# Six extra short TensorE passes, in two groups, in the last third of a two-layer streaming encoder

## The chip, the cores and the metric

The kernel runs on one core of a Trainium2 chip. The metric is the device time of one execution in microseconds (us). The input arrays are laid out on the host beforehand and are no part of the time.

## The reference, cut to what matters

272 tokens (16 learned ones and 256 of the input) of width 2048 pass two layers. Layer 0 is a Mamba-2 mixer and a SwiGLU feed-forward. Then one shared K/V is projected, and layer 1 is a stick-breaking attention and a second SwiGLU feed-forward. The part around the change is this:

```python
def stick_breaking_attention(u, w_q, k, v, w_o):
    ...
    return o @ w_o

def swiglu(u, w_gate_up, w_down):
    gu = u @ w_gate_up
    return (jax.nn.silu(gu[..., :FFN_HIDDEN]) * gu[..., FFN_HIDDEN:]) @ w_down

# layer 1
h = h + stick_breaking_attention(u, sb_w_q[j], k_shared, v_shared, sb_w_o[j])
h = h + swiglu(rmsnorm(h, norm_ffn[layer]), ffn_gate_up[layer], ffn_down[layer])
return rmsnorm(h, final_norm)[:, N_META:]
```

All of it is float32; D_MODEL is 2048 (16 blocks of 128), FFN_HIDDEN is 5632 (44 blocks of 128).

## The kernel before, in words

Activations lie transposed: 128 features on the partitions, tokens along the free dimension (272 of them in layer 0 and in K/V, 256 from the query projection on). Every weight matrix is streamed once from HBM in chunks of 128 x 1024 (`load`, tile `raw`, 5 buffers, on SyncE's queue).

To keep float32 accuracy at the speed of the fp32r type, each weight chunk is split by `halves` into a rounded part `hi` (ScalarE, L105, 5 buffers) and a remainder `lo` (VectorE, L107, 4 buffers), and the activations are kept as two such parts as well (`pair`, `split_scaled`). One 128 x 128 block of a product is then three matmul passes in PSUM (`mac`): hi by the low part of x (L120), hi by its high part (L121), lo by its high part (L122). Each pass has its own weight load (LDWEIGHTS), also of 128 x 128.

`project` makes one output tile: 16 blocks (44 in the down projection) by three passes, all into one PSUM tile of the pool `pp` (tag "pp", 4 buffers). `project_block` makes several output tiles at once, one chunk of eight blocks of each in turn, and calls `pump()` after each chunk; `pump` advances the generators in `side`, which hold the small work of the last attention heads (`attend`: transposes L551 to L553 and L576 to L580, scores L560 and L561, the product with V L586 to L588). `rstd` makes a row norm with plain float32 matmuls (L180) in a PSUM tile of the pool `pr` (one buffer).

The end of the kernel, which the change touches, is in this order: for each of 16 heads the K, V and query tiles with `attend` woven in (the query tile reads `uq`, 256 columns); then the attention's output projection `w_o` on `ob` (256 columns), whose first `FILLERS` = 4 tiles go through `project_block` and the other 12 through `project`, one by one; then `ffn(1, ...)` on `u` (256 columns), whose first four tiles (gate 0, up 0, gate 1, up 1) go through `project_block` with `rstd` after the first half, then gate and up of m = 2 to 43 through `project`, then the down projection on `hid`; then a short tail with the final norm.

TensorE takes its passes in program order. Nothing else orders the work around the change than the program order and the waits on the buffers named above. The ten passes at L202 at the very start of the kernel write a `pr` tile (`wake`) that nobody reads either.

Of the kernel before, what the change touches and what calls it, by code (L numbers as in the profile page):

```python
# [6 lines left out]
F32 = mybir.dt.float32  # L7
# [6 lines left out]
P = 128  # L14
# [22 lines left out]
FILLERS = 4  # L37
# [8 lines left out]
def trunk(tc, a, out):  # L46
    nc = tc.nc
    V, S, PE = nc.vector, nc.scalar, nc.tensor

    with tc.tile_pool(name="const", bufs=1) as cp, \  # L50
# [38 lines left out]
        def nm(s):  # L89
            uid[0] += 1  # L90
            return f"{s}_{uid[0]}"


        def load(src, k0, n, m=P):
            raw = wp.tile([P, LC, P], F32, tag="raw", name=nm("raw"), bufs=RAW)
            b0 = k0 // LC * LC
            b1 = min(b0 + LC, src.shape[0] // (P * m))
            piece = src[b0 * P * m:b1 * P * m].rearrange("(p k c) -> p k c", p=P, c=m)
            nc.sync.dma_start(raw[:, :n, :m], piece[:, k0 - b0:k0 - b0 + n, :])
            return raw  # L100


        def halves(raw, n, m=P):
            hi = wp.tile([P, WC, P], F32R, tag="hi", name=nm("hi"), bufs=5)
            S.copy(hi[:, :n, :m], raw[:, :n, :m])  # L105
            lo = wp.tile([P, WC, P], F32R, tag="lo", name=nm("lo"), bufs=4)
            V.tensor_tensor(out=lo[:, :n, :m], in0=raw[:, :n, :m],  # L107
                            in1=hi[:, :n, :m].bitcast(F32), op=ALU.subtract)
            return hi, lo


        def pair(pool, K, n, pad, step, tail=0, **kw):
            t = pool.tile([P, pad + 2 * K * step + tail], F32R, **kw)
            t = t[:, pad:pad + 2 * K * step].rearrange("p (s k t) -> p s k t", s=2, t=step)
            return [t[:, i, :, :n] for i in range(2)]

        def mac(ps, hi, lo, j, x, k, first, last, m=P):
            n = x[0].shape[-1]
            wh, wl, xh, xl = hi[:, j, :m], lo[:, j, :m], x[0][:, k, :], x[1][:, k, :]
            PE.matmul(ps[:, :n], wh, xl, start=first, stop=False)  # L120
            PE.matmul(ps[:, :n], wh, xh, start=False, stop=False)  # L121
            PE.matmul(ps[:, :n], wl, xh, start=False, stop=last)  # L122

        def project(src, x, m=P, o=None, then=None):
            K = x[0].shape[1]
            if o is None:
                o = pp.tile([P, 512], F32, tag="pp", name=nm("pp"))
            o = o[:m]
            for k0 in range(0, K, WC):
                c = min(WC, K - k0)  # L130
                if k0 % LC == 0:
                    raw = load(src, k0, min(LC, K - k0), m)
                hi, lo = halves(raw[:, k0 % LC:], c, m)
                for j in range(c):
                    mac(o, hi, lo, j, x, k0 + j, k0 + j == 0, k0 + j == K - 1, m)
                if k0 == 0 and then:
                    then()
            return o

        def project_block(srcs, x, then=None):  # L140
            K = x[0].shape[1]
            pss = [pp.tile([P, 512], F32, tag="pp", name=nm("pp")) for _ in srcs]
            for k0 in range(0, K, WC):
                c = min(WC, K - k0)
                for ps, src in zip(pss, srcs):
                    hi, lo = halves(load(src, k0, c), c)
                    for j in range(c):
                        mac(ps, hi, lo, j, x, k0 + j, k0 + j == 0, k0 + j == K - 1)
                    pump()
                if k0 == 0 and then:  # L150
                    then()
            return pss

        def times(dst, ps, r):
            V.tensor_tensor(out=dst, in0=ps[:, :r.shape[-1]], in1=r, op=ALU.mult)  # L155

        def residual(hm, ps):
            V.tensor_tensor(out=hm, in0=ps[:, :hm.shape[-1]], in1=hm, op=ALU.add)  # L158

        def split_scaled(dst, k, src, gcol):  # L160
            S.activation(dst[0][:, k, :], src, AF.Identity, scale=gcol)
            V.scalar_tensor_tensor(out=dst[1][:, k, :], in0=src, scalar=gcol,
                                   in1=dst[0][:, k, :].bitcast(F32),
                                   op0=ALU.mult, op1=ALU.subtract)
# [10 lines left out]
        def rstd(dst, acc, width, more=()):  # L175
            n = acc.shape[-1]
            ps = prp.tile([P, 512], F32, tag="pr", name=nm("pr"))
            parts = [acc, *more]
            for i, part in enumerate(parts):
                PE.matmul(ps[:, :n], ones, part, start=i == 0, stop=i == len(parts) - 1)  # L180
            sd = sp.tile([P, T], F32, tag="ms", name=nm("sd"), bufs=1)[:, :n]
            S.activation(sd, ps[:, :n], AF.Sqrt, bias=epst, scale=1.0 / width)
            V.reciprocal(dst, sd)
# [14 lines left out]
        u = pair(upool, KD, T, PAD["u"], TP, 16, tag="u", name="u0")  # L198
# [4 lines left out]
        for k, c in PIECES:  # L203
# [11 lines left out]
            hi, lo = halves(raw, GT * c)  # L215
# [6 lines left out]
        with tc.tile_pool(name="ssd0", bufs=1) as q0, \  # L222
# [13 lines left out]

            with tc.tile_pool(name="dtp", bufs=1) as dq:
                psd = project(a["w_dt"], u, m=NH, o=ptp.tile([P, 512], F32, tag="pt", name=nm("pt")),
                              then=lambda: rstd(rB, acc, D))[:, :T]
                for j in range(GT):  # L240
# [237 lines left out]
            u = pair(upool, KD, T, PAD["u"], TP, 16, tag="u", name="u1")  # L478
# [4 lines left out]
        def ffn(layer, u, t0, finish):  # L483
            n = T - t0
            with tc.tile_pool(name=f"ffn{layer}", bufs=1) as fp, \
                    tc.tile_pool(name=f"fft{layer}", bufs=2) as ft:
                gu, dn = a["w_gu"][layer], a["w_down"][layer]
                r = rB[:, t0:]
                pre = project_block([gu[0], gu[KF], gu[1], gu[KF + 1]], u,
                                    lambda: rstd(r, acc[:, t0:], D))  # L490
                for f0, f1 in PARTS[layer]:
                    hid = pair(fp, PARTS[layer][0][1], n, PAD["hid"][layer], TP if layer == 0 else SEQ,
                               tag="hid", name=nm(f"hid{layer}"))
                    hid = [v[:, :f1 - f0] for v in hid]
                    for m in range(f0, f1):
                        gt = ft.tile([P, n], F32, tag="gt", name=nm("gt"))
                        times(gt, pre.pop(0) if pre else project(gu[m], u), r)
                        S.activation(gt, gt, AF.Silu)
                        ut = ft.tile([P, n], F32, tag="ut", name=nm("ut"))
                        times(ut, pre.pop(0) if pre else project(gu[KF + m], u), r)  # L500
                        V.tensor_tensor(out=ut, in0=ut, in1=gt, op=ALU.mult)
                        S.copy(hid[0][:, m - f0, :], ut)
                        V.tensor_tensor(out=hid[1][:, m - f0, :], in0=ut, in1=hid[0][:, m - f0, :].bitcast(F32),
                                        op=ALU.subtract)
                    done = finish if f1 == KF else lambda m, ps: residual(h[:, m, t0:], ps)
                    srcs = [dn[m][f0 * P * P:f1 * P * P] for m in range(KD)]
                    for i, ps in enumerate(project_block(srcs[:FILLERS], hid)):
                        done(i, ps)
                    for m in range(FILLERS, KD):
                        done(m, project(srcs[m], hid))  # L510
# [3 lines left out]
        def finish0(m, ps):  # L514
# [4 lines left out]
            sumsq(acc, h[:, m, :], m == 0)  # L519

        ffn(0, u, 0, finish0)
        ukv = ukv[0]


        with tc.tile_pool(name="att1", bufs=1) as b1p, \
# [5 lines left out]
            ob = pair(b1p, KD, SEQ, PAD["ob"], SEQ, name="ob")  # L531
# [62 lines left out]
            pre = project_block([a["w_kv"][0], a["w_kv"][KD]], ukv, lambda: rstd(rB, acc, D))  # L594
# [17 lines left out]
            u = pair(upool, KD, SEQ, PAD["u2"], SEQ, tag="u", name="u2")  # L612

            def finish_o(m, ps):
                hm = h[:, m, META:]
                residual(hm, ps)
                split_scaled(u, m, hm, gam[:, 3, m:m + 1])
                sumsq(acc[:, META:], hm, m == 0)
# [1 line left out]
            for i, ps in enumerate(project_block([a["w_o"][m] for m in range(FILLERS)], ob)):  # L620
                finish_o(i, ps)
            for m in range(FILLERS, KD):
                finish_o(m, project(a["w_o"][m], ob))

        sqz = cp.tile([P, SEQ], F32, name="sqz")

# [23 lines left out]
        pr = pp.tile([P, 512], F32, tag="pp", name="prow")  # L650
# [3 lines left out]
        m = 0  # L654
        for n in (1, 3, 4, 4, 4):
            o = wp.tile([P, LC, P], F32, tag="raw", name=nm("o"), bufs=RAW)
            o = o.rearrange("p k c -> p (k c)")[:, :n * SEQ].rearrange("p (k t) -> p k t", t=SEQ)
# [73 lines left out]
```

## Time and profile before

| | us |
|---|---|
| three timed runs | 2665.23, 2666.65, 2697.81 |
| their median | 2666.65 |
| the profiled execution's own time | 2696.9 |
| span of its trace | 2695.2 |
| TensorE busy in it | 2681.5 (99%) |
| granted TensorE clock in it (mean) | 0.998 |

The profiled execution is one more execution, beside the three timed ones. The span is the time from the first to the last instruction; 1.7 us lie outside it. TensorE's busy time counts each pass from its modelled start to its modelled end, and passes overlap, so that a pass of 281 ns can follow another after 118 ns; the distance from start to start is what adds up to the time.

### The profile page before, as it was taken

Reading aid. Unit: us, or ns where it says so; the run is one execution under the profiler, and the core shown is the slowest. Engines: PE = TensorE matmul, PEld = TensorE weight load, DVE = VectorE, ACT = ScalarE, POOL = GpSimd, SP = SyncE. Lnnn points to the kernel's source line nnn. Section 1 sums busy time; section 2 is a strip of 40 time slices with the busy share of each in tenths; the row PEclk is TensorE's granted clock in tenths of the full one; section 3 lists DMA queues with packets and bytes.
Section 4 is the critical chain, followed back from the end, with each engine's and each line's share of the span. In section 5 each row is a group of like instructions: output and inputs, shape, how many; then the busy total and the mean of one; then the engine's idle time right before and its main releaser. Section 6 shows DMA issues by size and latency. Waiting matters only on the chain.

```text
span 2695.2 us, 52245 instructions
## 1 busy us (share of the span) xinstructions
PE 2681.5 (99%) x22112; PEld 2666.0 (99%) x22112; DVE 1609.6 (60%) x2236; ACT 1307.3 (49%) x1792; POOL 5.5 (0%) x22
## 2 busy tenths in 40 slices
PE   9999999999999999999999999999999999999998
PEld 9999999999999999999999999999999999999998
DVE  8777767667755554445555655555655555554544
ACT  7766556645544443334444544444544444443443
POOL 0000000000000000000000000000000000000000
PEclk9999999999999999999999999999999999999999
DMA  6655655554555555555555555455565556655653
GB/s 227 221 178 179 179 177 178 184 172 158 172 180 175 180 178 180 178 175 180 180 168 177 187 163 157 159 157 165 182 191 186 187 187 188 186 188 171 196 189 129
DMA packets 156234, 481.23 MB, mean 179 GB/s; under 512 B 18720, under 2 KB 39776, under 8 KB 156000
## 3 DMA queue, kind: packets, MB, share of 16 engines
q1 hardware_dynamic: 155712, 477.62, 56.4%
q8 instruction: 173, 2.83, 0.4%
q14 instruction: 61, 0.50, 0.1%
q10 hardware_dynamic: 288, 0.28, 0.0%
HBM read 475.67 MB, written 2.17 MB: 177 GB/s over the span
## 4 chain that ended last, share of the span: by engine, by line
PE 98%; DVE 1%; ACT 0%; issue 0%; DMA 0%; DVEq 0%; SPq 0%
PE pp L122 31%; PE pp L120 31%; PE pp L121 31%; PE py L432 1%; PE py L434 1%; PE pt L359 0%; DVE lo L107 0%; PE po L586 0%; PE po L587 0%; PE psc L561 0%; PE pr L180 0%; DVE ca L316 0%; DVE o L658 0%; PE psc L560 0%; PE pc L392 0%
## 5 line engine op out<-in xcount | busy, mean ns | idle before, releaser
L105 ACT CAST hi<-raw 128x1024 fp32r<-128x1024 f32 (+1 forms) x899 | 928.3, 1034 | 1210.5 <-PE pp L121 981.5
L107 DVE TENSOR_TENSOR lo<-raw,hi 128x1024 fp32r<-128x1024 f32 (+1 forms) x899 | 1075.6, 1197 | 457.9 <-PE pp L122 225.3
L120 PE MATMUL pp<-u,hi 128*128 128x272 f32 (+1 forms) x4064 | 1158.8, 285 | 0.5 <-ACT hi L105 0.5
L122 PE MATMUL pp<-u,lo 128*128 128x272 f32 (+1 forms) x4064 | 1157.2, 285 | 0.0
L121 PE MATMUL pp<-u,hi 128*128 128x272 f32 (+1 forms) x4064 | 1156.5, 285 | 0.0
L121 PEld LDWEIGHTS pp<-u,hi 128*128 128x128 f32 x4064 | 770.5, 190 | 0.2
L120 PEld LDWEIGHTS pp<-u,hi 128*128 128x128 f32 x4064 | 764.5, 188 | 1.3 <-ACT hi L105 0.7
L122 PEld LDWEIGHTS pp<-u,lo 128*128 128x128 f32 x4064 | 764.3, 188 | 0.8 <-DVE lo L107 0.4
L121 PE MATMUL pp<-hid,hi 128*128 128x272 f32 (+1 forms) x1408 | 399.5, 284 | 0.0
L120 PE MATMUL pp<-hid,hi 128*128 128x272 f32 (+1 forms) x1408 | 399.5, 284 | 0.0
L122 PE MATMUL pp<-hid,lo 128*128 128x272 f32 (+1 forms) x1408 | 399.5, 284 | 0.0
L121 PEld LDWEIGHTS pp<-hid,hi 128*128 128x128 f32 x1408 | 267.8, 190 | 0.0
L120 PEld LDWEIGHTS pp<-hid,hi 128*128 128x128 f32 x1408 | 264.7, 188 | 0.0
L122 PEld LDWEIGHTS pp<-hid,lo 128*128 128x128 f32 x1408 | 264.7, 188 | 0.0
L120 PE MATMUL pp<-y,hi 128*128 128x272 f32 x512 | 149.1, 291 | 0.0
L120 PE MATMUL pp<-ukv,hi 128*128 128x272 f32 x512 | 148.2, 289 | 0.0
L122 PE MATMUL pp<-y,lo 128*128 128x272 f32 x512 | 148.1, 289 | 0.0
L121 PE MATMUL pp<-y,hi 128*128 128x272 f32 x512 | 147.6, 288 | 0.0
L122 PE MATMUL pp<-ukv,lo 128*128 128x272 f32 x512 | 146.7, 287 | 0.0
L121 PE MATMUL pp<-ukv,hi 128*128 128x272 f32 x512 | 146.7, 287 | 0.0
L158 DVE TENSOR_TENSOR h<-pp,h 128x272 f32<-128x272 f32 (+1 forms) x128 | 55.6, 435 | 125.4 <-PE pp L122 123.9
L155 DVE TENSOR_TENSOR gt<-pp,rB 128x272 f32<-128x272 f32 (+1 forms) x88 | 38.1, 433 | 140.4 <-PE pp L122 140.3
(218 smaller groups left out, 2597.3 us busy)
## 6 DMA issues: line engine op xcount, KB each, us to landing
raw<-w_gu SPq DMA_DIRECT2D x352, 512.0 KB, 3.6
raw<-w_down SPq DMA_DIRECT2D x160, 512.0 KB, 3.6
raw<-w_in SPq DMA_DIRECT2D x152, 512.0 KB, 3.7
raw<-w_out SPq DMA_DIRECT2D x64, 512.0 KB, 3.7
raw<-w_kv SPq DMA_DIRECT2D x64, 512.0 KB, 3.6
raw<-w_q SPq DMA_DIRECT2D x32, 512.0 KB, 3.6
raw<-w_o SPq DMA_DIRECT2D x32, 512.0 KB, 3.6
raw<-w_down SPq DMA_DIRECT2D x32, 256.0 KB, 2.6
```

Source lines behind the costliest of these rows:

```text
L105: S.copy(hi[:, :n, :m], raw[:, :n, :m])
L107: V.tensor_tensor(out=lo[:, :n, :m], in0=raw[:, :n, :m], in1=hi[:, :n, :m].bitcast(F32), op=ALU.subtract)
L120: PE.matmul(ps[:, :n], wh, xl, start=first, stop=False)
L121: PE.matmul(ps[:, :n], wh, xh, start=False, stop=False)
L122: PE.matmul(ps[:, :n], wl, xh, start=False, stop=last)
L155: V.tensor_tensor(out=dst, in0=ps[:, :r.shape[-1]], in1=r, op=ALU.mult)
L158: V.tensor_tensor(out=hm, in0=ps[:, :hm.shape[-1]], in1=hm, op=ALU.add)
L432: PE.matmul(py[i * HD:(i + 1) * HD, c0:c1], xd[b][:, 2 * j + i, :], gm[b][:, 2 * j + i, :], start=b < 2, stop=b != 1)
L434: PE.matmul(py[:, T:T + T - OQ], xw[:, 2 * j:2 * j + 2, :], cb[:, OQ:T], start=True, stop=True)
```

## The change

A helper `beat` is added. It takes a PSUM tile of the pool `pr` and runs three passes of 128 columns into it, each with `start` and `stop` set: block 0 of `hi` by the first 128 columns of block 0 of x's high part, the same by the low part, block 0 of `lo` by the high part. `project` gets a flag `beats`, by which it calls `beat` after the first chunk's `halves` and ahead of its first `mac`. The flag is set in two places: at the fifth tile of `w_o` (m = 4, the first after the block of four) and at gate tile m = 2 of the second feed-forward (the fifth tile there, again the first after the block of four). Nothing reads the tile.

```diff
+        def beat(hi, lo, x):
+            b = prp.tile([P, 512], F32, tag="pr", name=nm("beat"))
+            for w, s in ((hi, 0), (hi, 1), (lo, 0)):
+                PE.matmul(b[:, :P], w[:, 0, :], x[s][:, 0, :P], start=True, stop=True)
+
-        def project(src, x, m=P, o=None, then=None):
+        def project(src, x, m=P, o=None, then=None, beats=False):
...
                 hi, lo = halves(raw[:, k0 % LC:], c, m)
+                if k0 == 0 and beats:
+                    beat(hi, lo, x)
                 for j in range(c):
                     mac(o, hi, lo, j, x, k0 + j, k0 + j == 0, k0 + j == K - 1, m)
...
-                        times(gt, pre.pop(0) if pre else project(gu[m], u), r)
+                        times(gt, pre.pop(0) if pre else project(gu[m], u, beats=(layer, m) == (1, 2)), r)
...
             for m in range(FILLERS, KD):
-                finish_o(m, project(a["w_o"][m], ob))
+                finish_o(m, project(a["w_o"][m], ob, beats=m == FILLERS))
```

## Rows read from the trace of the kernel before

**Rows 1.** The page's part 1: busy time, share, instructions by engine.

```profile
PE 2681.5 (99%) x22112; PEld 2666.0 (99%) x22112; DVE 1609.6 (60%) x2236; ACT 1307.3 (49%) x1792; POOL 5.5 (0%) x22
```

**Rows 2.** The page's chain that ended last, share by engine.

```profile
PE 98%; DVE 1%; ACT 0%; issue 0%; DMA 0%; DVEq 0%; SPq 0%
```

**Rows 3.** Busy time by stretch (PE and PEld first; PEclk third from the end).

```profile
1960.00:2660.00 700.00, 700.00 (x5946) 700.00 (x5945) 372.86 (x453) 303.31 (x368) 0.00 (x0) 1.00 0.60 187
```

**Rows 4.** TensorE's timeline, a query tile (start, duration).

```profile
1574.49 0.38 PE L588 MATMUL po<-ab,vb 128*128 128x128 f32 x2
...
1575.30 0.28 PE L122 MATMUL pp<-uq,lo 128*128 128x256 f32 x1
...
1580.06 0.28 PE L122 MATMUL pp<-uq,lo 128*128 128x256 f32 x1
```

**Rows 5.** Groups by shape over the whole span: passes of 256 columns.

```profile
L120 PE MATMUL pp<-u,hi 128*128 128x256 f32 x1408 | 395.8, 281 | 0.0
...
L120 PE MATMUL pp<-hid,hi 128*128 128x256 f32 x704 | 197.8, 281 | 0.0
...
L120 PE MATMUL pp<-ob,hi 128*128 128x256 f32 x256 | 72.3, 283 | 0.0
```

**Rows 6.** TensorE's timeline, the first query tile, after a V tile.

```profile
1535.62 0.28 PE L122 MATMUL pp<-ukv,lo 128*128 128x272 f32 x1
1535.75 0.28 PE L120 MATMUL pp<-uq,hi 128*128 128x256 f32 x1
...
1540.93 0.28 PE L122 MATMUL pp<-uq,lo 128*128 128x256 f32 x1
```

**Rows 7.** TensorE's timeline in w_o's block of four.

```profile
1847.68 0.62 PE L561 MATMUL psc<-kT,qT 128*128 128x272 f32 x2
...
1848.50 0.28 PE L120 MATMUL pp<-ob,hi 128*128 128x256 f32 x1
...
1850.88 0.28 PE L120 MATMUL pp<-ob,hi 128*128 128x256 f32 x1
1851.85 0.27 PE L576 MATMUL pa<-ident,sc 128*16 128x128 f32 x1 [0.69 <-DVE sc L572]
...
1855.97 0.38 PE L588 MATMUL po<-ab,vb 128*128 128x128 f32 x2
...
1856.31 0.28 PE L121 MATMUL pp<-ob,hi 128*128 128x256 f32 x1
...
1858.90 0.28 PE L122 MATMUL pp<-ob,lo 128*128 128x256 f32 x1
```

**Rows 8.** Timeline at the second feed-forward's norm, two engines' rows.

```profile
1946.64 0.59 PE L180 MATMUL pr<-acc,ones 128*128 128x256 f32 x2
...
1947.19 0.28 PE L121 MATMUL pp<-u,hi 128*128 128x256 f32 x1
1947.20 0.19 PEld L122 LDWEIGHTS pp<-u,lo 128*128 128x128 f32 x1
```

**Rows 9.** TensorE's timeline, eight short transposes, first and last.

```profile
1839.83 0.27 PE L576 MATMUL pa<-ident,sc 128*16 128x128 f32 x1
...
1840.59 0.27 PE L553 MATMUL pt<-ident,vT 128*128 128x128 f32 x1
```

**Rows 10.** TensorE's timeline, the kernel's first passes (L202).

```profile
1.12 4.50 PE L202 MATMUL wake<-ones 128*128 128x128 f32 x20 [1.12 <-DVE epst L71]
```

**Rows 11.** Groups by shape, 1860 to 1930 us: the two splitters.

```profile
L107 DVE TENSOR_TENSOR lo<-raw,hi 128x1024 fp32r<-128x1024 f32 x25 | 30.5, 1219 | 5.9 <-PE pp L122 5.9
L105 ACT CAST hi<-raw 128x1024 fp32r<-128x1024 f32 x26 | 27.3, 1050 | 36.7 <-PE pp L121 35.6 <-issue 1.1
```

**Rows 12.** Line 182 after 1900 us: durations, first and last start.

```profile
L182 ACT ACTIVATE sd<-pr,epst x1: 473/473/473, 1949.1 to 1949.1; 128x256 f32<-128x256 f32 x1
```

**Rows 13.** Timeline at the fifth tiles: of w_o, of the second feed-forward.

```profile
1867.50 0.28 PE L120 MATMUL pp<-ob,hi 128*128 128x256 f32 x1
...
1958.38 0.28 PE L120 MATMUL pp<-u,hi 128*128 128x256 f32 x1
```

## The prediction

> **What bounds the kernel.** The busy shares come first: TensorE is busy for 99% of the span, with as many weight loads as passes, and no other engine is above 60% [rows 1]. The chain of work that ended last says the same: 98% of it is TensorE [rows 2]. So every nanosecond between the starts of two passes is a nanosecond of the kernel, and the next question is how far apart the starts are. A busy time can't tell that, since passes overlap; counts in a stretch and the timeline can.
>
> From 1960 to 2660 us, inside the second feed-forward, 5946 passes touch a stretch of 700 us at a granted clock of 1.00 [rows 3]. Two or three of these began before it, so the starts are 700 / 5943.5 = 117.8 ns apart. Now a query tile: from 1575.30 to 1580.06 us lie 42 steps, 4.76 / 42 = 113.3 ns each [rows 4]. These are passes of the same shape, 128 x 128 weights by 256 columns, at the same clock. So one stream of work can run in **two rhythms**, a short one of 113.3 and a long one of 117.8 ns, 4.45 ns apart, and neither has any wait in it.
>
> What chooses between them? Not the data alone. The very first query tile reads the same `uq`, but follows a V tile without a break, and runs 44 steps in 5.18 us, 117.7 ns each [rows 6]. In the block of four `w_o` tiles both occur on the same `ob`: after the scores of a head 21 steps take 2.38 us (113.3 ns), and after the last value product 22 steps take 2.59 us (117.7 ns) [rows 7]. In each case the rhythm holds until something else than these passes comes between. The last such thing in the trace ahead of the end is the norm of the second feed-forward; it leaves the long rhythm as it was [rows 8], and 735 us then pass in it.
>
> The passes of 256 columns in the final stretch, on `ob`, `u` and `hid`, are 3 x (256 + 1408 + 704) = 7104 [rows 5]. In the long rhythm they cost 7104 x 4.45 ns = 31.6 us more than in the short one. The profiled execution took 2696.9 us, 30.2 us over the median of the timed runs, and the three timed runs are two at 2665 to 2667 and one at 2698. Nothing else of this size is at hand: I read the three numbers as two executions with the short rhythm from about the end of the block of four on, and one, like the profiled one, with the long rhythm. That is inferred from the sum; no trace of a short execution is shown.
>
> **The change, part by part.** Nothing is removed or moved, and no DMA is added. Added are two groups of three passes of 128 columns, each with its weight load, at the fifth tile of `w_o` (1867.50 us in this trace) and at the fifth tile of the second feed-forward (1958.38 us) [rows 13].
>
> Their own price. No fp32r pass of 128 columns is in the trace. Nearest are the transposes with 128 columns: seven steps in 0.76 us, 109 ns each [rows 9]. That is a little under the short rhythm of the longer passes (113.3 ns), as it should be if the weight load of 128 columns, the same in both, sets the pace. I take 113 ns: 6 x 0.113 = 0.7 us. The lower bound is nothing, if the passes end a bubble that is there anyway. The upper one is the row of the first ten products of 128 columns in plain float32, two instructions each, 4.50 us in all [rows 10], 0.45 us a product: 6 x 0.45 = 2.7 us.
>
> What they wait for. A group reads `lo` in its third pass, as the first block did without it, so at most some hundredths of a us earlier. The splitters run ahead as far as their buffers let them: between 1860 and 1930 us VectorE's idle time ahead of `lo` is all wait for TensorE to free a buffer, and so is 35.6 of 36.7 us on ScalarE [rows 11]. With four `lo` buffers a chunk of 24 passes (2.8 us) is ready some 3 x 2.8 - 1.2 = 7 us before its use, so this costs nothing. The PSUM tile of `pr` was last written by the norm at 1946.64 us [rows 8] and read by the square root at 1949.1 us for 0.47 us [rows 12], 9 us ahead of the second group; ahead of the first group the attention has no use of this pool. Without that cover it would be a wait of some tenths of a us, once. Behind the passes on TensorE stand only the products that would have run there; ScalarE, VectorE and the queue of loads get their buffers 0.7 us later and have spare time for it.
>
> What they do to the rhythm is the only term that matters, and its sign is open. Between the groups lie 576 passes on `ob` (12 tiles of 48) and 192 on `u` (4 tiles), after the second 3 x (1408 + 704) - 192 = 6144. At 4.45 ns that is 3.4 and 27.3 us. A switch from long to short in the profiled execution would give 2696.9 - 3.4 - 27.3 + 0.7 = 2666.9 us. In the two timed executions that I read as short there is nothing to win, and the median of the runs becomes 2666.65 + 0.7 = 2667.35 us. The two ways agree; I take the second, which rests on more executions, 2667.3 us.
>
> Why I lean to the short rhythm: in it a pass starts 113 ns after the one ahead, and each weight load starts just after the pass ahead has (the load at 1947.20 behind the pass at 1947.19 us [rows 8] shows how tightly the two follow each other). A pass of 128 columns needs less of the array's time and the same load, so in a group the load alone sets the pace, and a group that meets the short rhythm should leave it alone. A group that meets the long one breaks it, and the next block starts from the load's pace. Against it: breaks by other work end both ways. The transposes and the value product give the long rhythm on `ob`, the value product gives the short one on `uq`, the scores the short one on both, the norm leaves the long one [rows 4, 7, 8]. By kinds that is about half and half, from which the lean above takes me to some six in ten for a lasting short rhythm.
>
> The Trainium skill says in "TensorE: Matmul & The Clock Gate", Part 2 (What happens when you issue a matmul), that a reorder window pulls weight loads ahead of running matmuls. Taken at its word, a stream would regain any lost phase and have no rhythm to choose; the trace speaks against it, since 735 us of [rows 3] stay at 117.8 ns where [rows 4] run at 113.3 ns. The same page's back-to-back section gives 81 ns for a 128-column pair of load and matmul; six of them would make an estimate of 0.5 us in place of 0.7 us.
>
> **The rivals.**
> - *No memory across the group.* The stream finds its rhythm from what came earlier and the group changes nothing after itself. For it: the norm at 1946.64 us came between and the long rhythm went on [rows 8]. Then executions stay mixed as before: two of three at 2667.4, one at 2698 us, and the median is most often 2667.4 us. It is the case in which the change does nothing but cost its passes. The reorder window of the Trainium skill's page on TensorE (Part 2) would lead to it too.
> - *The second group lands in the long rhythm each time.* Its place is the first block after 1958.38 us, its price 6144 x 4.45 ns = 27.3 us against a short execution, with the first group's 3.4 us the same way: 2667.4 + 30.7 = 2698.1 us, slower by 1.2%. It decides as soon as more than half of the executions leave the group in the long rhythm. For it: after 128-column work `ob` took the long rhythm [rows 7]. Against it: no load is delayed by a long moving read in the group.
> - *The two groups differ.* First long, second short: 2667.4 + 3.4 = 2670.8 us. The reverse: 2667.4 + 27.3 = 2694.7 us.
> - A third rhythm above 121 ns after the second group would be needed for a loss over 2% (53 us on the 768 + 6144 = 6912 passes is 7.7 ns each, on top of 113.3); no 256-column stretch read here is above 117.8 ns.
>
> **How the numbers follow.** The forecast, 2667.3 us, holds for the short rhythm after both groups in most executions, whether the groups bring it or keep it: chance 0.55. No memory: 0.17, three quarters of it at the same time. Long after the second group: 0.20. Groups that differ: 0.06. Anything else: 0.02. The short cases alone reach from 2664 us (the fastest run, 2665.2, with groups that cost nothing, less a us for the spread between runs) to 2669.4 us (the upper price, 2.7 us, on the median), and hold about 0.68; for eight in ten the long case has to be inside, which ends at 2697.81 + 0.7 = 2698.5 us, so the range is 2664 to 2699 us. A measurement of this kernel can tell about 2% from no change, here 53 us; both rhythms lie within it, so "same" has 0.97, a gain over 2% would need over 53 us where all passes in the short rhythm give 31.6 us at most, 0.01, and a loss over 2% needs the third rhythm, 0.02.
>
> **What the changed profile would show.** Right: six passes of 128 columns, some 110 ns apart, ahead of the fifth tiles; then starts 113.3 ns apart to the end (some 6178 passes touch a stretch of 700 us in place of 5946), and a profiled time near 2667 us. Wrong: the same groups and then 117.8 ns, a rhythm that changes with no group near, or a wait on `lo` or on the `pr` tile ahead of a group. The weakest step is the reading of the timed runs as two rhythms of the same stretch; if the 30 us come from elsewhere, the groups can't touch it and the time is one of the two old ones.

## The result and the profile after

The changed kernel took 2666.60 us (median of 20 runs, 2665.18 to 2668.43). The kernel before, run 20 times beside it, took 2696.07 us (2664.93 to 2697.81). The ratio is 0.9928, 95% interval 0.9901 to 0.9956, so the change is faster by 0.7%, with the interval clear of 1 but under the 2% at which a kernel would count as faster here. The two medians differ by more, 29.5 us, because the 20 runs of before fall into two heaps with nothing between them: 7 at 2664.9 to 2666.7 us and 13 at 2695.9 to 2697.8 us. All 20 runs of the changed kernel lie in one heap, where the lower one of before is. The means, 2685.8 and 2666.6 us, give the ratio.

The profiled execution of the changed kernel took 2666.77 us. The page's busy time by engine and its chain that ended last, against [rows 1, 2]:

```profile
span 2665.1 us, 52257 instructions
PE 2650.4 (99%) x22118; PEld 2635.0 (99%) x22118; DVE 1606.7 (60%) x2236; ACT 1307.7 (49%) x1792; POOL 5.5 (0%) x22
...
PE 98%; DVE 1%; ACT 0%; DMA 0%; issue 0%; DVEq 0%; SPq 0%; ACTq 0%
```

The six passes are there (22118 against 22112), TensorE still holds the whole chain, and it is busy 31 us less with more passes. The busy time by stretch, inside the second feed-forward, against [rows 3]:

```profile
1960.00:2640.00 680.00, 680.00 (x6002) 680.00 (x6002) 373.24 (x455) 307.32 (x372) 0.00 (x0) 1.00 0.63 192
```

Less the two or three passes that began ahead of the stretch, the starts are 680 / 5999.5 = 113.3 ns apart, at the same granted clock of 1.00 as the 117.8 ns of before. The rows by shape say where the 4.45 ns show. In the changed kernel:

```profile
L121 PE MATMUL pp<-u,hi 128*128 128x256 f32 x1333 | 367.9, 276 | 0.0
L122 PEld LDWEIGHTS pp<-u,lo 128*128 128x128 f32 x1333 | 250.2, 188 | 0.0
L121 PEld LDWEIGHTS pp<-u,hi 128*128 128x128 f32 x1333 | 250.2, 188 | 0.0
```

and in the kernel before, from 1960 to 2660 us:

```profile
L121 PE MATMUL pp<-u,hi 128*128 128x256 f32 x1340 | 376.5, 281 | 0.0
L121 PEld LDWEIGHTS pp<-u,hi 128*128 128x128 f32 x1339 | 257.1, 192 | 0.0
L122 PEld LDWEIGHTS pp<-u,lo 128*128 128x128 f32 x1340 | 251.5, 188 | 0.0
```

In the short rhythm every weight load is given 188 ns and every pass 276; in the long one a pass has 281, and one load of each three, always at the same line within a stretch, 192 ns. What makes that load longer no run shows.

TensorE's timeline around the first group, which begins at 1867.87 us (columns: start, duration), shows where the change comes:

```profile
1865.75 0.28 PE L120 MATMUL pp<-ob,hi 128*128 128x256 f32 x1
...
1867.75 0.28 PE L122 MATMUL pp<-ob,lo 128*128 128x256 f32 x1
1867.87 0.33 PE L128 MATMUL beat<-ob,hi 128*128 128x128 f32 x2
1868.04 0.28 PE L128 MATMUL beat<-ob,lo 128*128 128x128 f32 x1
1868.15 0.34 PE L120 MATMUL pp<-ob,hi 128*128 128x256 f32 x1
...
1868.80 0.28 PE L122 MATMUL pp<-ob,lo 128*128 128x256 f32 x1
...
1869.48 0.28 PE L122 MATMUL pp<-ob,lo 128*128 128x256 f32 x1
```

Ahead of the group 17 steps take 2.00 us (117.6 ns), as at the end of [rows 7]; behind it, from 1868.80 us on, six take 0.68 us (113.3 ns). This execution came to the fifth tile in the long rhythm and left the group in the short one. Its norm at 1944.40 us did not end that, and the second group met the short rhythm and left it alone:

```profile
1955.05 0.28 PE L120 MATMUL pp<-u,hi 128*128 128x256 f32 x1
...
1955.62 0.28 PE L122 MATMUL pp<-u,lo 128*128 128x256 f32 x1
1955.73 0.33 PE L128 MATMUL beat<-u,hi 128*128 128x128 f32 x2
1955.90 0.27 PE L128 MATMUL beat<-u,lo 128*128 128x128 f32 x1
...
1956.18 0.28 PE L121 MATMUL pp<-u,hi 128*128 128x256 f32 x1
```

Five steps in 0.57 us (114 ns) stand ahead of it. From L122 at 1955.62 to L121 at 1956.18 us lie 0.56 us, where two steps of the short rhythm would take 0.23: the three passes cost 0.33 us, both groups 0.7 us.

### The profile page after: what moved, and what is told of

Read it like the earlier page. It is cut to its first block, busy times and chain, and to the rows that moved or that the text cites. A ratio compares the mean times of both kernels' runs of the same rounds, so it can differ in the third digit from the quotient of the medians.

```text
span 2665.1 us, 52257 instructions
## 1 busy us (share of the span) xinstructions
PE 2650.4 (99%) x22118; PEld 2635.0 (99%) x22118; DVE 1606.7 (60%) x2236; ACT 1307.7 (49%) x1792; POOL 5.5 (0%) x22
## 4 chain that ended last, share of the span: by engine, by line
PE 98%; DVE 1%; ACT 0%; DMA 0%; issue 0%; DVEq 0%; SPq 0%; ACTq 0%
PE pp L120 31%; PE pp L122 31%; PE pp L121 31%; PE py L440 1%; PE py L442 1%; PE pt L367 0%; DVE lo L107 0%; PE po L594 0%; PE po L595 0%; PE psc L569 0%; PE pr L188 0%; DVE ca L324 0%; DMA et<-cumD 0%; DMA raw<-w_first 0%; DVE o L666 0%
## 5 line engine op out<-in xcount | busy, mean ns | idle before, releaser
L122 PE MATMUL pp<-u,lo 128*128 128x272 f32 (+1 forms) x4064 | 1150.2, 283 | 0.0
L121 PE MATMUL pp<-u,hi 128*128 128x272 f32 (+1 forms) x4064 | 1149.5, 283 | 0.0
L122 PEld LDWEIGHTS pp<-u,lo 128*128 128x128 f32 x4064 | 764.2, 188 | 0.8 <-DVE lo L107 0.4
L121 PEld LDWEIGHTS pp<-u,hi 128*128 128x128 f32 x4064 | 764.7, 188 | 0.2
L121 PE MATMUL pp<-hid,hi 128*128 128x272 f32 (+1 forms) x1408 | 396.0, 281 | 0.0
L122 PE MATMUL pp<-hid,lo 128*128 128x272 f32 (+1 forms) x1408 | 396.0, 281 | 0.0
L122 PEld LDWEIGHTS pp<-hid,lo 128*128 128x128 f32 x1408 | 264.8, 188 | 0.0
L121 PEld LDWEIGHTS pp<-hid,hi 128*128 128x128 f32 x1408 | 264.8, 188 | 0.0
L122 PE MATMUL pp<-y,lo 128*128 128x272 f32 x512 | 148.1, 289 | 0.0
L121 PE MATMUL pp<-y,hi 128*128 128x272 f32 x512 | 147.7, 288 | 0.0
L122 PE MATMUL pp<-ukv,lo 128*128 128x272 f32 x512 | 146.7, 287 | 0.0
L121 PE MATMUL pp<-ukv,hi 128*128 128x272 f32 x512 | 146.7, 287 | 0.0
```

## The experiments

Each kernel below is the changed one with the edit shown, except where it says that it is the kernel before. The tile that the added passes write is read nowhere. Runs of the kernel before stand beside each set of kernels; how many of them were long differed from set to set, each on a chip of its own: 3 of 25 beside the first three, 5 of 24, 13 of 25, and 1 of 13 beside the last. So a time alone says little, and the traces and the sums carry the reading.

**One group alone.** The first kernel has only the group at the fifth `w_o` tile:

```diff
-  project(gu[m], u, beats=(layer, m) == (1, 2))
+  project(gu[m], u)
```

> Only the group at the fifth w_o tile is left; the second feed-forward has none. Theory A (a group of short passes puts the stream into the 113.3 ns rhythm, and it stays there until other work breaks in; the norm's break keeps it): every execution short, 2666.3 us, 0.3 us under the changed kernel. Theory B (each group acts only until the next break, and the norm's break decides anew): the second feed-forward is mixed as before, so executions near 2666 and near 2693 us.

It took 2665.79 us (10 runs, 2665.25 to 2666.75, none long; ratio 0.9982, interval 0.9950 to 1.0013). As theory A has it. With 3 long of 25 beside it, ten short ones are weak by themselves.

The second kernel has only the later group:

```diff
-  finish_o(m, project(a["w_o"][m], ob, beats=m == FILLERS))
+  finish_o(m, project(a["w_o"][m], ob))
```

> Only the group at the fifth tile of the second feed-forward is left. Theory A: w_o runs in either rhythm as before, everything after the group at 113.3 ns: 2666.3 us where w_o was short already, 2666.3 + 3.4 = 2669.7 us where it was long. Theory B (it is the early group that counts): mixed, near 2666 and near 2696 us.

It took 2666.34 us (10 runs; ratio 0.9987, 0.9955 to 1.0018): seven at 2665.3 to 2666.6 us, three at 2669.4, 2670.2 and 2670.3 us, none near 2697. A middle heap at 2669.7 us was what theory A expected of executions that are long through `w_o` and short after the group, and the kernel before has none there. So the later group acts alone as well.

**Passes of 256 columns in the groups.**

```diff
-                PE.matmul(b[:, :P], w[:, 0, :], x[s][:, 0, :P], start=True, stop=True)
+                PE.matmul(b[:, :SEQ], w[:, 0, :], x[s][:, 0, :SEQ], start=True, stop=True)
```

> Both groups stay, but their six passes have 256 columns, as the products around them; they write the unread tile of the other PSUM pool all the same. Theory A (shortness matters, since then the weight load alone sets the pace): the long rhythm runs on through the groups, executions mixed near 2666.6 and 2697 us, and a trace that comes in long stays at 117.8 ns behind the group. Theory C (any change of PSUM tile or any break of the threefold order resets the rhythm): always short, 2666.8 us.

Nine of ten runs at 2665.5 to 2666.5 us, one at 2697.52 us (median 2665.76; ratio 0.9985, 0.9939 to 1.0031). The one long run speaks for theory A, since an execution stayed long past both groups; one is little, and the transposes below were meant to give more of them.

**The kernel before again, for a short trace.**

> The kernel before once more, for its trace. If the two times of it are the two rhythms of one stretch, an execution near 2666 us has 113.3 ns per pass from about the block of four w_o tiles to the end, and one near 2697 us 117.8 ns; the stages ahead are alike. If the 30 us come from elsewhere (loads, waits, the clock), the passes of 256 columns are alike in both.

It took 2664.78 us, and its trace has the short rhythm in the same stretch, by the same row as above:

```profile
1960.00:2640.00 680.00, 680.00 (x6003) 680.00 (x6002) 373.88 (x455) 308.67 (x374) 0.00 (x0) 1.00 0.62 192
```

6003 passes touch 680 us, 6002 in the changed kernel. So one kernel has both rhythms, and the 30 us are that. Its timeline also shows where the two executions part:

```profile
1850.36 0.28 PE L120 MATMUL pp<-ob,hi 128*128 128x256 f32 x1
1851.33 0.27 PE L576 MATMUL pa<-ident,sc 128*16 128x128 f32 x1 [0.69 <-DVE sc L572]
...
1851.79 0.37 PE L121 MATMUL pp<-ob,hi 128*128 128x256 f32 x1
1851.99 0.28 PE L122 MATMUL pp<-ob,lo 128*128 128x256 f32 x1
...
1852.23 0.28 PE L121 MATMUL pp<-ob,hi 128*128 128x256 f32 x1
...
1852.91 0.28 PE L121 MATMUL pp<-ob,hi 128*128 128x256 f32 x1
```

Up to here both are alike: long at 1841 us, short behind the scores [rows 7]; so is every other trace of this document. Then the last head's transposes wait 0.69 us for VectorE's softmax row. After them this execution takes six steps in 0.68 us (113.3 ns). The profiled one of before took the long rhythm at the same place, 15 steps in 1.77 us (118 ns), and kept it through the value product and the norm [rows 7, 8]:

```profile
1852.51 0.28 PE L122 MATMUL pp<-ob,lo 128*128 128x256 f32 x1
...
1854.28 0.28 PE L122 MATMUL pp<-ob,lo 128*128 128x256 f32 x1
```

**Transposes in place of the first group, no second group.**

```diff
-            for w, s in ((hi, 0), (hi, 1), (lo, 0)):
-                PE.matmul(b[:, :P], w[:, 0, :], x[s][:, 0, :P], start=True, stop=True)
+            for i in range(8):
+                PE.transpose(b[:, :P], ident, ident)
...
-  project(gu[m], u, beats=(layer, m) == (1, 2))
+  project(gu[m], u)
```

> In place of the first group stand eight transposes of a constant (128 columns each, about 109 ns), as those that opened the long rhythm on ob at 1840 us in every trace so far; there is no second group. Theory A (short passes of any kind bring the short rhythm): always short, 2666 + 0.9 = 2667 us. Theory D (the kind of break decides, and transposes end in the long rhythm): always long from the fifth w_o tile on, 6912 passes x 4.45 ns more, about 2697 us, also where the stretch ahead was short.

All nine runs took the long time: 2696.87 us (2696.28 to 2698.87; ratio 1.0096, 1.0060 to 1.0132), slower than before, whose runs beside it were short in 19 of 24. The timeline and the stretches of its trace:

```profile
1866.33 0.28 PE L120 MATMUL pp<-ob,hi 128*128 128x256 f32 x1
...
1866.89 0.28 PE L122 MATMUL pp<-ob,lo 128*128 128x256 f32 x1
1867.01 1.04 PE L128 MATMUL beat<-ident 128*128 128x128 f32 x8
...
1868.12 0.28 PE L122 MATMUL pp<-ob,lo 128*128 128x256 f32 x1
...
1869.18 0.28 PE L122 MATMUL pp<-ob,lo 128*128 128x256 f32 x1
```

```profile
1858.00:1866.00 8.00, 8.00 (x73) 8.00 (x73) 5.76 (x10) 5.17 (x9) 0.00 (x0) 1.00 0.55 186
1960.00:2660.00 700.00, 700.00 (x5945) 700.00 (x5945) 373.04 (x452) 302.97 (x368) 0.00 (x0) 1.00 0.59 187
```

Short ahead of the eight (five steps in 0.56 us, 73 passes in 8 us), long behind them (nine steps in 1.06 us), and long to the end. So a break can also turn a short stream long, and passes of 128 columns are not short-rhythm passes as such: theory A fell in the form "short passes of any kind". This gave a way to bring streams to the second group in the long rhythm.

**The transposes, then the change's own second group.** Here, and in the next kernels of this kind, the `w_o` site has the eight transposes and the second site what the diff shows.

```diff
+            if x is ob_ref[0]:
+                for i in range(8):
+                    PE.transpose(b[:, :P], ident, ident)
+                return
             for w, s in ((hi, 0), (hi, 1), (lo, 0)):
```

> The eight transposes at the fifth w_o tile, and the change's own group of three short passes at the fifth tile of the second feed-forward. If the transposes bring the long rhythm and the group ends it each time: 2666 + 0.9 + 3.4 + 0.3 = about 2670.5 us in every execution. If the group has no power over a long rhythm: about 2697 us. If the transposes bring nothing: 2667 us.

2670.21 us (10 runs, 2667.51 to 2670.93; ratio 0.9997, 0.9965 to 1.0029). Nine lie at 2669.6 to 2670.9 us, where long through `w_o` and short after the group was expected; the tenth, 2667.51 us, is what an execution that was short behind the transposes too would take. In the trace the switch stands at the group:

```profile
1957.70 0.28 PE L121 MATMUL pp<-u,hi 128*128 128x256 f32 x1
...
1958.53 0.28 PE L122 MATMUL pp<-u,lo 128*128 128x256 f32 x1
1958.65 0.34 PE L132 MATMUL beat<-u,hi 128*128 128x128 f32 x2
1958.82 0.28 PE L132 MATMUL beat<-u,lo 128*128 128x128 f32 x1
...
1959.22 0.28 PE L122 MATMUL pp<-u,lo 128*128 128x256 f32 x1
...
1959.90 0.28 PE L122 MATMUL pp<-u,lo 128*128 128x256 f32 x1
```

Seven steps in 0.83 us (some 118 ns) ahead, six in 0.68 us (113.3 ns) behind.

**The transposes, then three passes of 256 columns.**

```diff
-                PE.matmul(b[:, :P], w[:, 0, :], x[s][:, 0, :P], start=True, stop=True)
+                PE.matmul(b[:, :SEQ], w[:, 0, :], x[s][:, 0, :SEQ], start=True, stop=True)
```

> The eight transposes at the fifth w_o tile, and a group of three passes of 256 columns into the unread tile at the fifth tile of the second feed-forward. Theory A (shortness is what ends the long rhythm): long to the end, about 2697.5 us. Theory C (a break of the order or of the PSUM tile is enough): about 2670.5 us, as with the short group.

2697.49 us (10 runs; ratio 1.0088, 1.0048 to 1.0129): eight at 2696.8 to 2698.8 us, two at 2666.7 and 2668.3 us. By their times the eight stayed long past the group, so a different PSUM tile and a break of the order of three are not enough: theory C fell, and in a group of these three passes their shortness is needed. The trace fell on one of the two others, and was a surprise:

```profile
1858.00:1866.00 8.00, 8.00 (x70) 8.00 (x70) 6.09 (x10) 5.30 (x9) 0.00 (x0) 1.00 0.54 169
1880.00:1930.00 50.00, 50.00 (x443) 50.00 (x442) 32.67 (x48) 25.84 (x38) 0.00 (x0) 1.00 0.62 191
```

It came to the transposes long (70 passes in 8 us, where the first kernel with transposes has 73) and left them short (443 in 50 us, where [rows 3] have 50 / 0.1178 = 424). So the eight transposes don't always end in the long rhythm, as theory D said. Nor do they simply exchange the two. The trace of the kernel with two passes, further down, has the same eight transposes; it too came to them long, and it left them long (427 passes in 50 us):

```profile
1858.00:1866.00 8.00, 8.00 (x70) 8.00 (x69) 5.52 (x9) 4.93 (x9) 0.00 (x0) 1.00 0.52 164
1880.00:1930.00 50.00, 50.00 (x427) 50.00 (x426) 31.34 (x45) 24.98 (x36) 0.00 (x0) 1.00 0.61 187
```

All four traces that came to the transposes short left them long; of the two that came long, one left short and one long. What decides between these two is open.

**The transposes, then one short pass, or two.**

```diff
-            for w, s in ((hi, 0), (hi, 1), (lo, 0)):
+            for w, s in ((hi, 0),):
```

> The eight transposes at the fifth w_o tile, then only one short pass (the first of the three) at the fifth tile of the second feed-forward. If one load-paced step is enough to end the long rhythm: about 2670.2 us, as with the group of three. If the stretch has to be longer: the executions that the transposes made long stay long, about 2697.5 us.

Neither outcome alone: four runs at 2669.3 to 2670.7 us and six at 2693.4 to 2694.8 us (median 2693.5; ratio 1.0012, 0.9962 to 1.0063). The trace is one of the four, and has the switch from long to short at the pass, within some six passes (45 passes in 5 us ahead, 6003 in 680 us behind):

```profile
1950.00:1955.00 5.00, 5.00 (x45) 5.00 (x44) 4.83 (x6) 3.69 (x4) 0.00 (x0) 1.00 0.47 170
1960.00:2640.00 680.00, 680.00 (x6003) 680.00 (x6002) 373.34 (x455) 306.33 (x370) 0.00 (x0) 1.00 0.63 193
```

The six lie about 3 us under the long heap of the kernel before. Short from the transposes to the second site and long from there is 2665.4 (the short runs beside it) + 0.9 for the transposes + 0.1 for the pass + 27.3 + 0.5 (the five chunks of 24 between the last head's transposes and the fifth tile, long) = 2694.2 us; long all through would be 2665.4 + 1.0 + 27.3 + 3.4 + 0.5 = 2697.6 us, and short behind both sites 2666.9; no run lies at either. So one pass seems to exchange the rhythms; the direction from short to long is worked out from these times, no trace shows it. With two passes, both by `hi`:

```diff
-            for w, s in ((hi, 0), (hi, 1), (lo, 0)):
+            for w, s in ((hi, 0), (hi, 1)):
```

> The eight transposes at the fifth w_o tile, then two of the three short passes (both by hi) at the fifth tile of the second feed-forward. One pass exchanged the two rhythms. If each pass exchanges them, two leave them as they were: long to the end where the transposes had made it long, about 2697.5 us, and 2667 us where they had made it short. If more than one pass in a row brings the short rhythm from either, as three do: 2670.3 and 2667 us, none above 2671 us.

By their times all ten runs were short behind the second site, and the trace was (45 passes in 5 us ahead, 6002 in 680 us behind): 2669.53 us (2665.94 to 2671.36; ratio 1.0004, 0.9979 to 1.0028), eight at 2669.2 to 2671.4 and two at 2665.9 and 2666.8 us. Two passes, like three, end in the short rhythm, from the long one in eight runs, one of them traced, and from the short one in two; so two passes are not two exchanges.

**The transposes, then three plain float32 products of 128 columns** (six passes of some 109 ns).

```diff
-            for w, s in ((hi, 0), (hi, 1), (lo, 0)):
-                PE.matmul(b[:, :P], w[:, 0, :], x[s][:, 0, :P], start=True, stop=True)
+            for i in range(3):
+                PE.matmul(b[:, :P], ones, ident, start=True, stop=True)
```

> The eight transposes at the fifth w_o tile, then three products of 128 columns in plain float32 (two passes each, some 109 ns a pass) at the fifth tile of the second feed-forward. Theory A refined (what ends the long rhythm is a stretch in which the weight load sets the pace; here the passes set it): not the group's result; the executions stay long, about 2698 us, or turn as after transposes. Theory A as first stated (any short pass does): about 2670.8 us.

Six runs at 2669.9 to 2671.3 us and four at 2694.1 to 2694.7 us (median 2670.84; ratio 0.9990, 0.9938 to 1.0043): the two heaps of the single pass. The trace, of the first heap, goes from long to short here as well (45 passes in 5 us ahead, 6003 in 680 us behind). So by the times these passes, which do not end in one rhythm from either side, exchange them. The refined theory A is borne out only in that they differ from the group.

**A group in the mixer's output projection.** The changed kernel with a third group, at tile 1 of the last output projection on `y`, in a tile of the pool `pp`:

```diff
-            b = prp.tile([P, 512], F32, tag="pr", name=nm("beat"))
+            b = pp.tile([P, 512], F32, tag="pp", name=nm("beat"))
...
-                    finish(m, project(src, ybuf[g0 // 2 % 2]))
+                    finish(m, project(src, ybuf[g0 // 2 % 2], beats=last and m == 1))
```

> The change, and a third group in the last quarter of the mixer's output projection (tile 1 of 16, 272 columns on y), where the trace of before has some 126 ns per pass all through, against 123.3 ns on u. If 126 is a long rhythm too and a group ends it: 720 passes x 2.8 ns = 2.0 us less, 0.3 us for the passes, so 2664.9 us. If it belongs to the data (where y lies): no change of spacing, 2666.9 us.

It took 2666.40 us in a single run. Ahead of and behind its group (at 696.29 us) the spacing is the same, 20 / 158 = 126.6 and 50 / 398 = 125.6 ns with the two passes that began before each stretch left out:

```profile
673.00:693.00 20.00, 20.00 (x160) 20.00 (x160) 14.79 (x22) 8.09 (x11) 0.00 (x0) 1.00 0.55 163
700.00:750.00 50.00, 50.00 (x400) 50.00 (x399) 37.39 (x62) 28.78 (x47) 0.00 (x0) 1.00 0.55 176
```

The slower spacing on `y` is not a rhythm that this group ended. Whether it comes from where `y` lies was not tried.

**The wait taken away.** The kernel before, no groups, with 16 unread passes of 256 columns ahead of the last head's transposes:

```diff
-        def project_block(srcs, x, then=None):
+        def project_block(srcs, x, then=None, fill=None):
...
+                    if fill is not None and ps is pss[fill] and k0 == 0:
+                        b = prp.tile([P, 512], F32, tag="pr", name=nm("fill"))
+                        for i in range(16):
+                            PE.matmul(b[:, :SEQ], hi[:, 0, :], x[0][:, 0, :], start=True, stop=True)
                     pump()
```

with `fill=2` at `w_o`.

> The kernel before, with sixteen unread passes of 256 columns ahead of the five transposes of the last head (in the block of four), so that the softmax row they wait for is there in time and the one wait of this stretch is gone. Theory W (the mixture of executions comes from that wait, whose end is not in step with TensorE): no mixture any more, all executions near 2666.5 us or all near 2697.5 us, 1 us of passes in place of 0.9 us of wait. Rival (the mixture comes from somewhere else): both times go on occurring, as in the runs of the kernel before beside it.

All ten runs were short, 2666.41 us (2665.47 to 2667.68; ratio 0.9936, 0.9895 to 0.9978), while the kernel before beside it was long in 13 of 25. At half and half, ten in a row come once in a thousand times. In the timeline the wait is gone:

```profile
1850.21 1.98 PE L152 MATMUL fill<-ob,hi 128*128 128x256 f32 x16
1852.02 0.27 PE L580 MATMUL pa<-ident,sc 128*16 128x128 f32 x1
...
1852.69 0.28 PE L121 MATMUL pp<-ob,hi 128*128 128x256 f32 x1
1852.81 0.28 PE L122 MATMUL pp<-ob,lo 128*128 128x256 f32 x1
```

The row of L580 has no idle time ahead of it, against 0.69 us for the same transposes above. So the mixture is gone with the wait, as theory W has it, and from 1841 us on the traces part at that wait and nowhere before it. Whether the end of the wait decides, or the sixteen added passes would have brought the short rhythm with the wait left in, was not separated. This kernel reaches the time of the changed one without a group.

## Why the prediction was wrong

The time itself was met, 2667.3 us forecast and 2666.60 measured, inside the range; what it was held against was not. **The step that failed** is the one that set what there was to win: "In the two timed executions that I read as short there is nothing to win, and the median of the runs becomes 2666.65 + 0.7 = 2667.35 us." It took three runs, two of them short, for the shares of a mixture. In 20 runs 13 were long, and the median of the 20 is 2696.07 us. So the change was forecast as nothing (2667.3 against 2666.65) and it was worth 29.5 us in the medians, 0.72% in the means. The profiled execution, a fourth draw and a long one, stood in the same text and was reconciled with the median and not counted with the runs: two of four. Nor is the share the kernel's alone. In three of the four sets of runs further up the median of the kernel before was 2665.4 to 2665.6 us, and against those a forecast of nothing would have stood; what sets the share in a set of runs is open.

The other steps, in their order:

- *Two rhythms of one stream.* Right: 117.8 ns [rows 3] and 113.3 ns in two traces of the same kernel at a clock of 1.00. They account for the 30 us, as inferred from 7104 passes; the third heap at 2670 us, long in `w_o` alone, is the 3.4 us of the 768 passes.
- *Price of the passes, 0.7 us.* Right, 0.33 us a group, or 110 ns a pass; the other estimate, 0.5 us, was too low. No wait on `lo` or on the PSUM tile appeared: in the final stretch the changed kernel's only wait of TensorE is the one it had, 0.7 us for the softmax row.
- *The rhythm holds until a break.* Right. The norm kept both rhythms, the long one [rows 8] and the short one.
- *A group ends the long rhythm and keeps the short one.* Right for groups of two and three: 20 runs of the changed kernel, 10 of the single early group, 10 and 10 behind the transposes. The reason given for it is only half shown. Passes of 256 columns in the same place leave a long rhythm long, by the times, so shortness counts; but one short pass and six plain passes turn a short stream long, by the times, and eight transposes do in four traces, so "the load sets the pace" is not a full account, and that the groups had three passes and not one was in part luck. The load that follows its pass within 0.01 us [rows 8] stands in a stretch of the long rhythm, so it is no sign of the short one. What in TensorE holds the rhythm stays open.
- *The reorder window.* The Trainium skill's page "TensorE: Matmul & The Clock Gate", Part 2, says that weight loads are pulled ahead of running matmuls, where the row groups don't conflict or the load goes to the background weight buffer. No run here shows whether the loads of this kernel meet either condition. The prediction took from it that a stream would make up a lost phase; the two executions of the same kernel stay at 113.3 and 117.8 ns to the end, so that does not happen here.
- *By kinds, breaks end both ways.* Too coarse, and in part misread: the value product does not give the long rhythm on `ob`, it keeps what it meets; in the trace of before the stream was long ahead of it (118 ns from 1852.51 us). What the stream was in counts, but is not all: eight transposes left one long stream short and another long. The five transposes of the last head end either way behind their wait for VectorE; with sixteen passes in place of the wait they ended one way in ten runs of ten.
- *The rivals.* No memory across the group: fell, by the trace at 1867.87 us. The second group long each time: fell, none of 20. Groups that differ: fell. A loss over 2%: nothing of the kind.

No kernel here is measurably better than the changed one: the early group alone (2665.79 us) and the filled wait (2666.41 us) lie within a us of it and were timed in other sets.

## What to carry to other kernels

When the runs of a kernel lie in two heaps, settle the share of each with more runs, in more than one set, before setting a change against their median; three say almost nothing. On a TensorE-bound stream, compare starts per stretch between executions, not busy shares: over 31 us were decided at a wait of 0.7 us here, because the stream behind it kept the rhythm it began with for 830 us. Two or three unread short passes at the head of a long stream, or the wait filled, bought that back for 0.3 to 1 us, and transposes in the same place turned short streams long, so such a group has to be tried from both rhythms.

## What the runs showed that was not expected

The same passes at the same granted clock have two stable spacings, 113.3 and 117.8 ns, and one of them lasts until the stream is broken. In the long one a single weight load of each three is 4 ns longer. Eight transposes turned four short streams long, one long stream short, and left another long. The share of long executions of one and the same kernel went from 1 in 13 to 13 in 20 between the sets of runs, so a comparison of medians across chips can show 30 us where nothing was changed.
